# Page numbers of six quads kept, latents one group of four pages sooner, memory squares summed on VectorE, and a later scaling of key tiles

## The chip, the cores and the metric

The kernel runs on one core of a Trainium2 chip. The metric is device time in microseconds (us) of one run. The core has TensorE (PE; its weight loads are shown as PEld), VectorE (DVE), ScalarE (ACT), GpSimd (POOL), and SyncE (SP), which here issues the DMAs. Each engine takes its own instructions in order and waits on semaphores for the others.

## What is computed

One step of a hybrid decoder layer for two groups that share the weights: a prompt of 1024 tokens and 8 samples of 4 new tokens, each with 4096 past tokens in 32 pages of 128. The parts that matter here, cut:

```python
def mla_keys_values(ckv_n, kpe, pos, w_uk, w_uv, g_qk_k):
    k_nope = (ckv_n @ w_uk).reshape(*lead, MLA_HEADS, QK_NOPE)
    v = (ckv_n @ w_uv).reshape(*lead, MLA_HEADS, V_HEAD)
    k = qk_rope(rms_norm(jnp.concatenate([k_nope, k_pe], axis=-1), g_qk_k), pos)

def one(args):                      # a sample's attention over its pages
    c_all = jnp.concatenate([pool_ckv[pages].reshape(PAST_LEN, KV_LORA), c1], axis=0)
    pe_all = jnp.concatenate([pool_kpe[pages].reshape(PAST_LEN, QK_ROPE), pe1], axis=0)
    k, v = mla_keys_values(c_all, pe_all, k_pos, w_uk, w_uv, g_qk_k)
    return masked_attend(q1, k, v, q_pos, k_pos)

def mem_kv(mem, g_mem_in, w_mk, w_mv, g_mk):
    hm = rms_norm(mem, g_mem_in)    # 256 memory tokens of width 1024
    k = rms_norm((hm @ w_mk).reshape(n, m, MEM_HEADS, MEM_HEAD_DIM), g_mk)
    v = (hm @ w_mv).reshape(n, m, MEM_HEADS, MEM_HEAD_DIM)
```

Around these stand a spatial gating group beside the attention, one output projection, cross-attention into the memory and a gated feed-forward network with a short convolution.

## The kernel before

All products are float32, split into a high and a low part and done as three products (`mm3`, line 185; the casts are L200 on ACT and L201 on DVE, with a scale L204 and L207). In order of time: projections; attention of the prompt; attention of the samples over their pages; keys and values of the memory (`mem_kv`); output projection; cross-attention; feed-forward. In the two attention stages the order on PE, ACT, DVE and POOL is the order of the code (`manual_schedule`). On SP, and everywhere from `mem_kv` on, a scheduler sets it by its own simulation, so an edit can move instructions well away from it.

**Prompt attention.** Eight heads run in two halves of four. For each group of four token tiles (512 tokens) a list of steps, made by `proj_group` with `part` and the generator `norm` (L901 to L930), makes queries and keys: products, sums of squares, a reciprocal root (`rsqrt_steps`, L232 to L246 on DVE, L248 to L255 on POOL), the scale of the queries (L911), then that of the keys (L925 on DVE, L926 on POOL for the rope part). `head_prep` transposes four tiles of k, then of q, on PE (L949) and splits them into kTh, kTl, qTh, qTl. A unit of attention then computes scores s (L185), row maxima on DVE (L979, L983, L985), exponentials on ACT (L988), transposes of the weights pr on PE (L996), copies of them on ACT (L998), products with v (L1011). The lists `extra[t]` hang further work onto step t of the units: steps of `norm`, and sums of feed-forward weights (`weight_sums`, L831 to L843, on POOL, with DMAs on SP).

**Samples.** A step n covers two pages; a quad Q is four pages, so two steps. `quad_pages` reads a quad's four page numbers into registers of SP (TENSOR_LOAD and eight register operations); `quad_load` starts four DMAs of latents (cT, 3 buffers) and, apart from them, four of another layout of the same pages (ck, 15 buffers). POOL makes the rotated rope part krq from cT (`quad_rot`, L1347 to L1349), ACT and DVE or POOL make the high and low parts ch (L1358) and cl (L1362), PE multiplies krq (L1377) and computes scores. `quad_sums` squares the rope part of ck on ACT (L1370). `pages_ahead` starts the first quads during the prompt attention. `batch_softmax` runs in numbered parts r: L1423 scales the scores, L1426 and L1452 take the maximum, r = 9 is a PE transpose (L1455), r = 10 two DVE operations (L1458, L1460), r = 11 a PE product that spreads the maximum (L1463), an ACT copy bc (L1465) and DVE's subtraction (L1466), the last is the exponential (L1468). Products with the values follow in `quad_pv` (L1475, L1477).

**Memory.** `mem_kv` begins within the end of the last batch. It casts the memory (mh, ml), makes four heads of keys (L1545), sums of squares of the memory per token for its norm (L1558 on ACT and L1560 on POOL over 8 slices of 128x256, then one-column products, L1581), and values in four calls `values(k)`, k = 0, 2, 4, 6. `behind(a, b)` makes a stand after b in order without a wait.

**Feed-forward.** Products of quarters (`block`, tiles A, X, F, E in PSUM), with weights split by `weights` (L2090, L2091). The first block has within it the norm of the tokens: hr by a reciprocal root on DVE, transposed on PE (`half_row`, L2044), copied by ACT (L2047). The tile A has two buffers, which `half_row` and the copy a of A (L2146) share.

Of the kernel before, what the change touches and what calls it, by code (L numbers as in the profile page):

```python
# [154 lines left out]
class Net:  # L155
# [502 lines left out]
    def phase2a(self):  # L658
# [86 lines left out]
        sums = [(i, z) for i in (NK, NK + 1, *range(NK)) for z in range(2)]  # L745
        times = (1, 2, 3, 4, 5, 7, 8, 9, 11, 12, 14, 15, 16, 25, 26, 27, 29, 30, 36, 37, 39, 40, 41, 43, 44, 46)
        for t, x in zip(times, sums):
# [19 lines left out]
        with tc.manual_schedule(engines={E.PE, E.Activation, E.DVE, E.Pool}):  # L767
# [9 lines left out]
            for f in norm[:2]:  # L777
                f()
            extra[0][:0] = norm[2:]
            extra[1][:0] = v1[3:]  # L780
            steps, outs, pend, V = [], {}, [], []
# [85 lines left out]
    def proj_group(self, p, pp, hf, i0, i1, s, c, tt=("tp", 4)):  # L867
# [32 lines left out]
        def norm():  # L900
# [4 lines left out]
            nc.vector.tensor_tensor(rk, rk, c["kss"][:tn, i0:i1].unsqueeze(2).broadcast_to([tn, m, 4]), ALU.add)  # L905
            rf = r.rearrange("p m z h -> p (m z h)")
            yield from self.rsqrt_steps(p, rf, rf, 1.0 / 96)
            yield
# [25 lines left out]
        it = norm()  # L934
        return [alloc] + qk + [lambda: next(it, 0)] * 6, [lambda i=i: part(i, 2) for i in range(i0, i1) if i < 8]

# [184 lines left out]
    def pages_ahead(self):  # L1121
# [8 lines left out]
        yield  # L1130
        self.quads = {Q: self.quad_load(None, Q) for Q in range(3)}
        self.rvs = {Q: self.quad_pages(Q) for Q in (3, 4)}
        yield
# [5 lines left out]
    def phase2b(self):  # L1139
# [74 lines left out]
        def steps(n0, n1):  # L1214
            for n in range(n0, n1):
                Q, v = n // 2, n - 16 - LAG
                if n >= 10 and n % 2 == 0 and Q + AHEAD < NB * 8:
                    quads[Q + AHEAD] = self.quad_load(p, Q + AHEAD)
# [13 lines left out]
                if n % 2 and 0 <= Q + 2 < NB * 8:  # L1232
                    self.quad_rot(Q + 2, quads[Q + 2], cosT, sinT)
                if n in (-1, 1, 3, 5, 7):
                    k = Q + 4
                    rvs[k] = rvs.get(k) or self.quad_pages(k)
                    quads[k] = self.quad_load(None, k, None, rvs[k])
                for k in {1: (0,), 3: (5, 1), 4: (2,), 5: (3,), 6: (4,), 8: (6, 7)}.get(n, ()):
                    self.quad_load(p, k, quads[k], rvs.get(k))
# [279 lines left out]
    def mem_kv(self, raws, wk0):  # L1519
# [7 lines left out]
        mh, ml = (self.t(p, [P, 8, 256], FR, x) for x in ("mh", "ml"))  # L1527
        acc = self.t(p, [P, 256], F32, "acc")
        mr = [r.rearrange("p (k n) -> p k n", k=4) for r in raws[1:3]]
# [3 lines left out]
        for h in range(4):  # L1533
# [20 lines left out]
            yield  # L1554
        for k in range(8):
            x = mr[k // 4][:, k % 4]
            s2 = acc if k == 0 else self.t(p, [P, 256], F32, "msq", 2)
            nc.scalar.activation(s2, x, AF.Square)  # L1558
            if k:
                nc.gpsimd.tensor_tensor(acc, acc, s2, ALU.add)  # L1560
        yield
        av = [self.t(pp, [P, 512], F32, f"v{i}") for i in range(2)]

        def values(k):
            wh, wl = (x.rearrange("p k n -> p (k n)").rearrange("p (k n) -> p k n", k=2) for x in self.stream(I["w_mv"][k // 2], 8))
            for i in range(2):
                t = slice(i * P, i * P + P)
                x = self.mm3(av[i], [tuple(x[:, t] for x in xs[k + e]) for e in range(2)],
                             [(wh[:, e], wl[:, e]) for e in range(2)], first=k == 0, last=k == 6)
                if k == 6 and i == 0:  # L1570
                    self.behind(x, self.spread)
# [8 lines left out]
        for i in range(2):  # L1580
            nc.tensor.matmul(st[:, 8 + i : 9 + i], acc[:, i * P : i * P + P], self.ones[:, :1], start=True, stop=True)  # L1581
        rt = self.t(p, [P, 2], F32, "rt")
# [872 lines left out]
```

## Time and profile before

| | |
|---|---|
| median of three runs | 1844.83 us (1842.12 to 1846.34) |
| the profiled execution | 1843.82 us, span 1842.1 us |
| mean granted clock of PE in it | 0.994 |
| prompt attention, about | 196 to 403 us |
| samples, about | 403 to 861 us |
| memory keys and values, about | 861 to 905 us |
| start of the feed-forward network, about | 1165 us |

Times in the trace are us from the span's start. A row of the timeline has start, length, engine, line, operation, output<-input and, in brackets, how long the engine was idle before it and what ended that. Several equal neighbours are one row with their count; matmuls overlap, so their lengths add up to more than their time. PEclk is the granted clock of TensorE as a share of full speed.

### The profile page before, as it was taken

The numbers are of one execution on the slowest core, as the hardware profiler recorded it, in microseconds if no ns is written. First come the engines' busy times: TensorE is split into PE (matmuls) and PEld (weight loads), VectorE is DVE, ScalarE is ACT, GpSimd is POOL, SyncE is SP. The second block draws the span as 40 slices with busy tenths as digits, with TensorE's granted clock in tenths as the row PEclk, the third lists the DMA queues.
The fourth block names the chain that finished last, engine by engine and source line by source line (L and its number), as shares of the span: only waits on it lengthen the run. The fifth ranks groups of instructions, "written<-read, shape, count | busy, mean of one in ns | idle before, by whom it ended". The sixth has DMA issues, their size and how long they took to land.

```text
span 1842.1 us, 39314 instructions
## 1 busy us (share of the span) xinstructions
PE 1809.4 (98%) x14222; PEld 1706.1 (93%) x14222; DVE 1354.1 (74%) x2805; ACT 922.9 (50%) x1916; POOL 697.1 (38%) x852
## 2 busy tenths in 40 slices
PE   9999999999999999999999999999999999999999
PEld 8999777779999999998899979999999999999999
DVE  7855767757778776786645666898888888878664
ACT  7435667766555555555433556533333333444442
POOL 1021555634444444453123110277766777400000
PEclk9999999999999999999999999999999999999999
DMA  8101353557767666654555155222222222495242
GB/s 324 42 25 66 109 194 109 183 167 210 222 191 194 193 176 188 181 168 145 160 161 181 62 179 169 98 82 70 93 82 70 70 82 75 140 328 173 78 154 77
DMA packets 153187, 261.18 MB, mean 142 GB/s; under 512 B 20897, under 2 KB 97538, under 8 KB 152994
## 3 DMA queue, kind: packets, MB, share of 16 engines
q1 hardware_dynamic: 152130, 257.63, 44.8%
q8 instruction: 112, 1.84, 0.4%
q10 hardware_dynamic: 864, 1.05, 0.2%
q14 instruction: 81, 0.66, 0.1%
HBM read 212.79 MB, written 45.82 MB: 140 GB/s over the span
## 4 chain that ended last, share of the span: by engine, by line
PE 73%; DVE 5%; issue 4%; ACT 2%; POOL 2%; DMA 1%; SPq 1%; DVEq 0%; POOLq 0%; ACTq 0%
PE s L185 16%; PE d L185 12%; PE b L185 8%; PE F L185 7%; PE E L185 7%; PE X L185 7%; PE A L185 3%; PE y L185 2%; PE o L1011 2%; PE tp L996 1%; PE tp L185 1%; PE o L1477 1%; PE tp L949 1%; PE t L185 1%; ACT pr L988 1%
## 5 line engine op out<-in xcount | busy, mean ns | idle before, releaser
L185 PE MATMUL s<-w2h,ch 128*128 128x288 f32 (+1 forms) x1024 | 304.4, 297 | 0.5 <-ACT S L1380 0.5
L185 PE MATMUL s<-w2h,cl 128*128 128x288 f32 (+1 forms) x1024 | 296.5, 290 | 3.3 <-POOL cl L1362 2.3
L185 PE MATMUL s<-w2l,ch 128*128 128x288 f32 (+1 forms) x1024 | 295.3, 288 | 0.0
L185 PEld LDWEIGHTS s<-w2h,ch 128*128 128x128 f32 x1024 | 193.3, 189 | 9.0 <-issue 2.5
L185 PEld LDWEIGHTS s<-w2h,cl 128*128 128x128 f32 x1024 | 193.1, 189 | 5.2 <-POOL cl L1362 3.9
L185 PEld LDWEIGHTS s<-w2l,ch 128*128 128x128 f32 x1024 | 193.5, 189 | 0.0
L1405 DVE TENSOR_REDUCE ss<-sq 128x16 f32<-128x1024 f32 x128 | 155.3, 1214 | 33.4 <-ACT sq L1402 33.0
L1362 POOL TENSOR_TENSOR cl<-cT,ch 128x512 fp32r<-128x512 f32 x64 | 83.8, 1310 | 126.7 <-ACT ch L1358 118.0
L1402 ACT ACTIVATE sq<-s 128x512 f32<-128x512 f32 x128 | 76.5, 598 | 89.5 <-PE s L185 89.5
L1399 ACT ACTIVATE sq<-s 128x512 f32<-128x512 f32 x128 | 76.7, 599 | 75.3 <-PE s L185 74.7
L200 ACT CAST a<-brb 128x528 fp32r<-128x528 f32 x77 | 48.8, 634 | 109.1 <-PE d L185 102.8
L185 PE MATMUL d<-a,w 128*128 128x264 f32 x768 | 95.2, 284 | 0.0
L185 PEld LDWEIGHTS d<-a,w 128*128 128x128 f32 x768 | 94.3, 188 | 0.0
L201 DVE TENSOR_TENSOR a<-brb,a 128x528 fp32r<-128x528 f32 x77 | 54.3, 707 | 53.7 <-ACT a L200 53.7
L2091 POOL TENSOR_TENSOR lo<-s,hi 128x1024 fp32r<-128x1024 f32 x20 | 63.8, 3190 | 45.7 <-ACT hi L2090 45.7
L185 PE MATMUL mm<-whi,xh 128*128 128x256 f32 (+3 forms) x272 | 77.2, 285 | 0.0
L185 PE MATMUL mm<-wlo,xh 128*128 128x256 f32 (+3 forms) x272 | 76.9, 285 | 0.1
L185 PE MATMUL mm<-whi,xl 128*128 128x256 f32 (+3 forms) x272 | 76.8, 286 | 0.0
L2146 ACT COPY a<-A 128x264 f32<-128x264 f32 x43 | 16.1, 374 | 118.4 <-PE A L185 114.4
L1358 ACT CAST ch<-cT 128x512 fp32r<-128x512 f32 x128 | 73.4, 626 | 2.1 <-DMA cT<-cT 2.1
L2212 POOL TENSOR_TENSOR cv<-cv,row 128x1056 f32<-128x1056 f32 x22 | 64.9, 2952 | 19.0 <-ACT cv L2211 19.0
L185 PE MATMUL d<-a,hi 128*128 128x264 f32 x552 | 72.0, 284 | 0.0
(746 smaller groups left out, 6350.3 us busy)
## 6 DMA issues: line engine op xcount, KB each, us to landing
cT<-cT SPq DMA_DIRECT2D x256, 160.0 KB, 2.7
ck<-ck SPq DMA_DIRECT2D x256, 144.0 KB, 3.3
raw<-w_up SPq DMA_DIRECT2D x44, 512.0 KB, 3.5
wsumd<-wsum SPq DMA_DIRECT2D x26, 512.0 KB, 3.6
actd<-cv SPq DMA_DIRECT2D x44, 264.0 KB, 2.3
brb<-actd SPq DMA_DIRECT2D x44, 264.0 KB, 5.7
wsum<-w_down SPq DMA_DIRECT2D x22, 512.0 KB, 3.4
raw<-wsumd SPq DMA_DIRECT2D x20, 512.0 KB, 3.6
```

Of the source, the lines that this page charges most:

```text
L185: x = self.nc.tensor.matmul(out, l, r, start=first and i == 0, stop=last and i == len(seq) - 1)
L200: first = {"act": nc.scalar.copy, "pool": nc.gpsimd.tensor_copy, "dve": nc.vector.tensor_copy}[eng](hi, src)
L201: low = lambda: nc.vector.tensor_tensor(lo, src, hi, ALU.subtract)
L949: nc.tensor.transpose(tp[:, j * P : j * P + P], s[x, g * 4 + j][:, h % 4], self.ident)
L1011: nc.tensor.matmul(u["o"][g : g + 64, o : o + m * P], s["v"][:, j, h % 4], th[:, z * P : (z + m) * P], start=j == 0, stop=b == len(banks) - 1,
L1358: nc.scalar.copy(d["h"][:, k], src[k])
L1362: (nc.vector if k else nc.gpsimd).tensor_tensor(d["l"][:, k], src[k], d["h"][:, k], ALU.subtract)
L1399: nc.scalar.activation(sq[:, 0], ps[:, :, n0 : n0 + 256], AF.Square)
L1402: nc.scalar.activation(sq[:, 1], pt.rearrange("p (e d) -> p e d", e=2), AF.Square)
L1405: yield lambda: nc.vector.tensor_reduce(s["ss"][:, g0 : g0 + 2].rearrange("p e (z h) -> p z e h", z=2), sq.rearrange("p z e (h d) -> p z e ...
L2091: eng.tensor_tensor(lo, src, hi, ALU.subtract)
L2212: nc.gpsimd.tensor_tensor(cv, cv, row, ALU.mult)
```

## The change

Five edits:

1. The first five weight sums of the prompt attention are hung one step later.
2. `norm` has one step more, between the sums and the reciprocal root. Of the second group (tokens 512 to 1023 of the first half) three steps now go to `extra[0]`, and what is left, the scaling of the key tiles, to `extra[1]`.
3. `pages_ahead` reads the page numbers of quads 0 to 5, and they are kept. Before, it read those of 0 to 4, and those of 0, 1 and 2 were read again for their ck.
4. Latents of quads 8, 9 and 10 are entered at n = 9, 11 and 13, no longer at 10, 12 and 14, and the ck of quads 5 to 10 are spread over n = 7 to 14.
5. In `mem_kv` ACT squares the memory in place, 128x1024 at a time, and DVE sums four slices in one reduction each; the two sums are added in PSUM by two more one-column products. The values of k = 4, no longer of k = 6, stand behind the spread of the maximum.

```diff
-        times = (1, 2, 3, 4, 5, 7, 8, 9, 11, 12, 14, 15, 16, 25, ...
+        times = (2, 3, 4, 5, 6, 7, 8, 9, 11, 12, 14, 15, 16, 25, ...
...
-            extra[0][:0] = norm[2:]
-            extra[1][:0] = v1[3:]
+            extra[0][:0] = norm[2:5]
+            extra[1][:0] = norm[5:] + v1[3:]
...
+            yield
             yield from self.rsqrt_steps(p, rf, rf, 1.0 / 96)
...
-        return [alloc] + qk + [lambda: next(it, 0)] * 6, ...
+        return [alloc] + qk + [lambda: next(it, 0)] * 7, ...
...
-        self.quads = {Q: self.quad_load(None, Q) for Q in range(3)}
-        self.rvs = {Q: self.quad_pages(Q) for Q in (3, 4)}
+        self.rvs, self.quads = {}, {}
+        for Q in range(6):
+            self.rvs[Q] = self.quad_pages(Q)
+            if Q < 3:
+                self.quads[Q] = self.quad_load(None, Q, None, self.rvs[Q])
...
-                if n >= 10 and n % 2 == 0 and Q + AHEAD < NB * 8:
+                if n >= 16 and n % 2 == 0 and Q + AHEAD < NB * 8:
...
-                if n in (-1, 1, 3, 5, 7):
+                if n in (-1, 1, 3, 5, 7, 9, 11, 13):
...
-                for k in {1: (0,), 3: (5, 1), 4: (2,), 5: (3,), 6: (4,), 8: (6, 7)}.get(n, ()):
+                for k in {1: (0,), 3: (1,), 4: (2,), 5: (3,), 6: (4,), 7: (5,), 9: (6,), 11: (7,), 12: (8,), 13: (9,), 14: (10,)}.get(n, ()):
                     self.quad_load(p, k, quads[k], rvs.get(k))
...
-        acc = self.t(p, [P, 256], F32, "acc")
+        acc = [self.t(p, [P, 256], F32, f"acc{z}") for z in range(2)]
...
-        for k in range(8):
-            x = mr[k // 4][:, k % 4]
-            s2 = acc if k == 0 else self.t(p, [P, 256], F32, "msq", 2)
-            nc.scalar.activation(s2, x, AF.Square)
-            if k:
-                nc.gpsimd.tensor_tensor(acc, acc, s2, ALU.add)
+        for x, s2 in zip(mr, acc):
+            nc.scalar.activation(x, x, AF.Square)
+            nc.vector.tensor_reduce(s2, x.rearrange("p k n -> p n k"), AX.X, ALU.add)
...
-                if k == 6 and i == 0:
+                if k == 4 and i == 0:
                     self.behind(x, self.spread)
...
-            nc.tensor.matmul(st[:, 8 + i : 9 + i], acc[:, i * P : i * P + P], self.ones[:, :1], start=True, stop=True)
+            for z in range(2):
+                nc.tensor.matmul(st[:, 8 + i : 9 + i], acc[z][:, i * P : i * P + P], self.ones[:, :1], start=z == 0, stop=z == 1)
```

The order of the instructions at three places. Line numbers of the changed kernel are up to 4 higher than before. First DVE in the prompt attention, from the scale of the queries (L911) of the second group to the low parts of its transposes; k is the key tile, pr and nm the masked scores and their row maximum. Before:

```order
L911 TENSOR_TENSOR rq_2427<-hr_2593,sq_tok_69 128x4x4
L925 TENSOR_TENSOR k_2594<-k_2594,hr_2593 128x8x64 x2
L979 ISA pr_432_2873,nm_2874<-s_2875,cmask_2419 128x384
L979 ISA nm_2874 128x1
L985 TENSOR_SCALAR nm_2874<-nm_2874,rq_2427 128x1
L979 ISA pr_435_2881,nm_2882<-s_2883,cmask_2419 128x512
L979 ISA nm_2882 128x1
L985 TENSOR_SCALAR nm_2882<-nm_2882,rq_2427 128x1
L201 TENSOR_TENSOR kTl_2710<-tp_2918,kTh_2709 96x512
L207 SCALAR_TENSOR_TENSOR qTl_2925<-tp_2926,ggq_2422,qTh_2924 96x512
```

And now:

```order
L912 TENSOR_TENSOR rq_2427<-hr_2593,sq_tok_69 128x4x4
L980 ISA pr_432_2870,nm_2871<-s_2872,cmask_2419 128x384
L980 ISA nm_2871 128x1
L986 TENSOR_SCALAR nm_2871<-nm_2871,rq_2427 128x1
L980 ISA pr_435_2878,nm_2879<-s_2880,cmask_2419 128x512
L980 ISA nm_2879 128x1
L986 TENSOR_SCALAR nm_2879<-nm_2879,rq_2427 128x1
L926 TENSOR_TENSOR k_2594<-k_2594,hr_2593 128x8x64 x2
L201 TENSOR_TENSOR kTl_2710<-tp_2910,kTh_2709 96x512
L207 SCALAR_TENSOR_TENSOR qTl_2917<-tp_2918,ggq_2422,qTh_2916 96x512
```

The scaling of the key tiles has moved behind the two maxima. Next DVE in `mem_kv`; lo are low parts of weights, S the scores of the last batch, ss their factor, mx the maximum, dg and bc its spread. Before:

```order
L201 TENSOR_TENSOR lo_14646<-raw_14643,hi_14645 128x1024
L201 TENSOR_TENSOR lo_14745<-raw_14742,hi_14744 128x1024
L201 TENSOR_TENSOR lo_14763<-raw_14760,hi_14762 128x1024
L1423 TENSOR_TENSOR S_12857<-S_12857,ss_12858 128x256
L201 TENSOR_TENSOR lo_14827<-raw_14824,hi_14826 128x1024
L1426 TENSOR_REDUCE mx_14401<-S_12857 128x32
L1452 TENSOR_TENSOR mx_14401<-mx_14401 128x32
L201 TENSOR_TENSOR lo_14881<-raw_14878,hi_14880 128x1024
L1458 TENSOR_REDUCE mm_14565<-m_14563 32x1
L201 TENSOR_TENSOR lo_14921<-raw_14918,hi_14920 128x1024
L1460 TENSOR_SCALAR dg_14567<-ident_60,mm_14565 32x32
```

And now:

```order
L201 TENSOR_TENSOR lo_14536<-raw_14533,hi_14535 128x1024
L1561 TENSOR_REDUCE acc_2105_14385<-ck_14160 128x256
L1561 TENSOR_REDUCE acc_2106_14386<-ck_14250 128x256
L201 TENSOR_TENSOR lo_14617<-raw_14614,hi_14616 128x1024
L1427 TENSOR_TENSOR S_12746<-S_12746,ss_12747 128x256
L201 TENSOR_TENSOR lo_14635<-raw_14632,hi_14634 128x1024
L1430 TENSOR_REDUCE mx_14290<-S_12746 128x32
L1456 TENSOR_TENSOR mx_14290<-mx_14290 128x32
L201 TENSOR_TENSOR lo_14701<-raw_14698,hi_14700 128x1024
L1462 TENSOR_REDUCE mm_14455<-m_14453 32x1
L1464 TENSOR_SCALAR dg_14457<-ident_60,mm_14455 32x32
```

The two reductions stand ahead of a weight cast; the low part of the next weight now comes after L1423 (L1427 there), and the subtraction (L1470 there) no longer follows the root of the memory's norm. Last PE in the same stage, where m<-ident,mx is the transpose of the maximum and m<-dg,ones its spread; v are the memory's values. Before, the end of `values(2)` and what follows it (the spread stands 17 rows further on, between the products of `values(6)`):

```order
L185 MATMUL v_2143_14741<-lo_14763,mh_14494 128x512
L185 MATMUL v_2143_14741<-hi_14762,ml_14495 128x512
L1579 MATMUL st_14493<-ones_61,sq_14606 128x1 x2
L1579 MATMUL st_14493<-ones_61,sq_14641 128x1 x2
L1579 MATMUL st_14493<-ones_61,sq_14676 128x1
L1455 MATMUL m_14563<-ident_60,mx_14401 32x128
L1579 MATMUL st_14493<-ones_61,sq_14676 128x1
L1581 MATMUL st_14493<-ones_61,acc_14496 128x1 x2
L185 MATMUL v_2142_14740<-hi_14826,mh_14494 128x512
```

And now, the transpose between the products of `values(0)`:

```order
L185 MATMUL v_2137_14613<-lo_14617,mh_14383 128x512
L185 MATMUL v_2137_14613<-hi_14616,ml_14384 128x512
L185 MATMUL v_2137_14613<-hi_14616,mh_14383 128x512
L1459 MATMUL m_14453<-ident_60,mx_14290 32x128
L185 MATMUL v_2137_14613<-lo_14617,mh_14383 128x512
L185 MATMUL v_2137_14613<-hi_14616,ml_14384 128x512
```

and, behind the twelve products of `values(2)`, the spread between the sums:

```order
L1580 MATMUL st_14382<-ones_61,sq_14496 128x1 x2
L1580 MATMUL st_14382<-ones_61,sq_14531 128x1 x2
L1467 MATMUL m_14459<-dg_14457,ones_61 128x32
L1580 MATMUL st_14382<-ones_61,sq_14566 128x1 x2
L1583 MATMUL st_14382<-ones_61,acc_2105_14385 128x1
L1583 MATMUL st_14382<-ones_61,acc_2106_14386 128x1
```

Both have moved ahead, the transpose by fourteen products of the values and the spread by eighteen. On SP the loads of cT for quads 6 to 10 now stand ahead of some loads of ck that they followed, with four readings of page numbers fewer among them, and at the start of the feed-forward network the scheduler puts the first transposes of hr (L2044) 35 products further back.

More of the change, by code (lines that the diff above doesn't have):

```diff
@@ L745, in phase2a @@
         sums = [(i, z) for i in (NK, NK + 1, *range(NK)) for z in range(2)]
-        times = (1, 2, 3, 4, 5, 7, 8, 9, 11, 12, 14, 15, 16, 25, 26, 27, 29, 30, 36, 37, 39, 40, 41, 43, 44, 46)
+        times = (2, 3, 4, 5, 6, 7, 8, 9, 11, 12, 14, 15, 16, 25, 26, 27, 29, 30, 36, 37, 39, 40, 41, 43, 44, 46)
         for t, x in zip(times, sums):
@@ L934, in proj_group @@
         it = norm()
-        return [alloc] + qk + [lambda: next(it, 0)] * 6, [lambda i=i: part(i, 2) for i in range(i0, i1) if i < 8]
+        return [alloc] + qk + [lambda: next(it, 0)] * 7, [lambda i=i: part(i, 2) for i in range(i0, i1) if i < 8]
     def head_prep(self, p, pp, h, s, c):
```

## The prediction

> **What bounds the kernel now.** I read the page first.
>
> ```profile
> span 1842.1 us, 39314 instructions
> PE 1809.4 (98%) x14222; PEld 1706.1 (93%) x14222; DVE 1354.1 (74%) x2805; ACT 922.9 (50%) x1916; POOL 697.1 (38%) x852
> ```
>
> TensorE (PE) is busy for 1809.4 of 1842.1 us, and the change takes no product away. It can only win what PE waits, and what PE loses when its clock is lowered. So the waits of PE come next (engine, line, what it waited for, total, times, longest); these four lie where the change works.
>
> ```profile
> PE o L1475 <- ACT S L1468: 2.3, 1, 2.3
> PE s L1377 <- POOL krq L1349: 2.3, 2, 1.8
> PE A L2044 <- DVE hr L246: 1.8, 1, 1.8
> PE m L1455 <- DVE mx L1452: 0.8, 1, 0.8
> ```
>
> No wait is longer than 2.3 us. Then I cut the trace into stretches around the waits, for the clock that was granted (columns: stretch, length, busy time and count of PE, PEld, DVE, ACT, POOL, then PEclk, DMA share, GB/s).
>
> ```profile
> 211.00:215.00 4.00, 1.93 (x10) 1.00 (x9) 2.15 (x5) 3.23 (x7) 3.69 (x6) 1.00 0.38 131
> 215.00:222.00 7.00, 7.00 (x26) 5.42 (x25) 4.22 (x15) 0.03 (x1) 1.11 (x2) 0.51 0.54 170
> 256.00:259.40 3.40, 2.32 (x18) 2.06 (x17) 1.64 (x7) 2.60 (x7) 2.92 (x4) 1.00 0.46 147
> 454.00:457.40 3.40, 1.61 (x14) 1.37 (x13) 2.96 (x7) 2.32 (x5) 2.40 (x4) 0.99 0.56 153
> 457.40:460.80 3.40, 3.40 (x17) 3.40 (x16) 3.40 (x4) 0.60 (x1) 3.32 (x5) 0.50 0.88 251
> 876.40:881.40 5.00, 5.00 (x23) 4.05 (x22) 0.46 (x3) 3.26 (x6) 4.35 (x9) 1.00 0.35 105
> 880.60:884.00 3.40, 2.58 (x21) 2.35 (x20) 3.01 (x5) 1.71 (x2) 0.32 (x2) 1.00 0.22 34
> 884.00:887.40 3.40, 3.40 (x11) 2.72 (x11) 3.12 (x13) 0.00 (x0) 0.00 (x0) 0.50 0.70 235
> 890.90:894.30 3.40, 1.17 (x6) 0.59 (x4) 3.06 (x14) 1.75 (x2) 0.00 (x0) 0.99 0.57 183
> 894.30:897.70 3.40, 3.32 (x32) 3.08 (x36) 0.79 (x4) 2.39 (x6) 0.00 (x0) 0.50 0.23 87
> 1173.60:1179.60 6.00, 6.00 (x51) 6.00 (x51) 3.10 (x3) 3.97 (x7) 0.88 (x2) 1.00 0.02 4
> ```
>
> Behind a 3.4 us stretch with 1.8 us or more of PE idle stands one at half clock: behind 457.4 and 894.3 for 3.4 us, behind 215.0 for 7 us. At 256.0 to 259.4 PE was idle 1.08 us and the clock stayed. At 880.6 to 884.0 0.82 us were idle, and half clock followed; there the trace has many one-column products, which may count little. At half clock half of the work is lost: 1.7 us behind each short one, 3.4 us behind 215.0. So a removed wait is worth itself, and 1.7 us more where it causes a dip.
>
> The Trainium skill ("TensorE: Matmul & The Clock Gate", the section on why this matters for kernels) sets the bar higher: avoid idle gaps over about 3 us, since one idle window halves the clock. The rows differ: dips here stand behind 0.8 to 2.3 us. By that rule only the idle time would be won, which is the first rival below.
>
> **The change, part by part.** Each sum is made against the profiled execution, 1843.82 us; that is 1.0 under the shown median of 1844.83.
>
> *Key tiles of the second token group (L925).* Moved behind the two row maxima of 384 and 512 columns (L979).
>
> ```profile
> 207.58 2.69 DVE L925 TENSOR_TENSOR k<-k,hr 128x512 f32<-128x512 f32 x2
> 210.01 0.73 PE L949 MATMUL tp<-ident,k 128*96 128x128 f32 x4
> 211.63 0.21 DVE L985 TENSOR_SCALAR nm<-nm,rq 128x1 f32<-128x1 f32 x1
> 213.16 0.68 ACT L204 ACTIVATE qTh<-tp,ggq 96x512 fp32r<-96x512 f32 x1
> 213.89 0.41 PE L185 MATMUL s<-kTh,qTh 96*128 96x320 f32 x1 [0.73 <-ACT qTh L204]
> ```
>
> The two maxima, which now stand between the end of L925 at 210.27 and the end of L985 at 211.84, come 2.7 us sooner, so the exponentials (L988) behind them and the waits of L996 for these fall. But the transposes of k (L949) read what L925 writes. It now ends the 1.6 us of the maxima later, at 211.9, and PE, in order, waits at L949 in place of L996. The last k transpose is then out at about 212.3, q's at 212.9, the two ACT casts end at 213.55: the scores start 0.3 us sooner than 213.89. L925 ran beside POOL work and may be shorter: 0.5. I take +0.4. The idle time is spread over 210.1 to 213.6, on both sides of the window edge at 211.6 (3.4 before 215.0), so the dip behind 215.0 may go (3.4 more) or stay; I leave it in the sum and give it to the range. Bounds: -0.5 to +3.9.
>
> The later groups have one more step each, so that three small DVE operations (L903 to L905, 0.6 us the first and an estimated 1.2 the three) come ahead of maxima that PE waits for, at two places.
>
> ```profile
> 292.67 0.60 DVE L903 TENSOR_TENSOR hr<-hr,sq_tok 128x16 f32<-128x16 f32 x1
> ```
>
> PE has slack of a few tenths there: -0.3, bounds -1.5 and 0. The five weight sums that are entered one step later keep their place on POOL and SP: 0.
>
> *Pages kept, latents sooner.*
>
> ```profile
> 415.35 0.59 SPq L1221 DMA_DIRECT2D ck<-b  x1
> 417.65 1.91 SPq L1330 DMA_DIRECT2D cT<-cT  x4
> 419.75 2.72 SPq L1334 DMA_DIRECT2D ck<-ck  x4
> 443.37 0.50 ACT L1370 ACTIVATE ksq<-ck 128x128 f32<-128x128 f32 x2
> 448.43 1.93 SPq L1330 DMA_DIRECT2D cT<-cT  x4
> 454.93 0.61 POOL L1347 TENSOR_TENSOR krq<-cT,cosT 128x128 f32<-128x128 f32 x1 [5.84 <-DMA cT<-cT]
> ```
>
> SP is one queue. A load of four pages takes 2.1 us of it (417.65 to 419.75), a reading of page numbers the 1.7 us from 415.94 to 417.65. Ahead of the latents (cT) of quad 8, issued at 448.43, four re-readings go (quads 0, 1, 2 and 5: 6.8 us), and the key load (ck) of quad 5 and one or two others move behind: some 8 to 12 us sooner, less where a buffer isn't free yet. POOL waited 5.84 us for quad 8's latents and PE 1.79 of them; both krq waits (2.3) go, and the dip behind 457.4 (1.7). Sum 4.0; I take 3.9, bounds 1.5 (an SP stall eats half) to 4.0. What is late next: ck of quad 5, read by L1370 at 443.37. It was issued at 419.75; now it goes behind quad 7's latents, an estimated 433 to 435, and lands near 438. ACT has 5 us in hand.
>
> *Memory squares.* Seven POOL additions, eight ACT squares go; two ACT squares of 128x1024 in place and two DVE reductions come.
>
> ```profile
> L1560 POOL TENSOR_TENSOR acc<-acc,msq x7: 727/734/741, 871.6 to 879.9; 128x256 f32<-128x256 f32 x7
> 599.62 1.22 DVE L1405 TENSOR_REDUCE ss<-sq 128x16 f32<-128x1024 f32 x1 [0.23 <-ACT sq L1402]
> 599.67 0.46 POOL L1348 TENSOR_TENSOR krq<-cT,sinT 128x128 f32<-128x128 f32 x1
> 867.78 1.39 POOL L249 TENSOR_TENSOR rqa<-rqa,rqx 128x64 f32<-128x64 f32 x1
> 880.95 0.43 DVE L1423 TENSOR_TENSOR S<-S,ss 128x256 f32<-128x256 f32 x1 [4.54 <-POOL ss L255]
> 883.10 0.19 DVE L1452 TENSOR_TENSOR mx<-mx 128x32 f32<-128x32 f32 x1
> 890.06 0.40 PE L1463 MATMUL m<-dg,ones 32*128 32x32 f32 x2
> 893.24 1.08 ACT L1468 ACTIVATE S<-S 128x1056 f32<-128x1056 f32 x1 [0.45 <-DVE rqh L245]
> 894.38 0.64 PE L1475 MATMUL o<-cn,S 128*32 128x257 f32 x1 [2.31 <-ACT S L1468]
> ```
>
> The additions stand between the small steps of POOL's reciprocal root; 7 x 0.73 = 5.1 us sooner its result reaches L1423: 875.8 instead of 880.95. A POOL step of 128x64 took 1.39 beside a DVE subtraction (the casts' low parts, L201), one of twice the size 0.46 within a DVE reduction; so the new reductions should not slow the chain. They are unpriced: the nearest row is 1.21 to 1.22 for 128x1024, strided an estimated double; at 2.4 each they still end by 875, ahead of the cast that values(0) needs. From L1423 to the maximum are 2.3 us: it is there at 878.1, and PE comes to the moved L1455 at 878.2 (8 products of 0.22 behind 876.4). The 0.82 us and the dip behind 884.0 go. PE then reaches the spread (L1463) at 882.2, ahead of the 24 last products (24 x 0.23 = 5.6 us) and 0.8 of small ones. From the spread to the exponential's start were 3.2 us (890.06 to 893.24); so much again and 1.08 make 886.5, and PE needs it at 888.6. So 2.31 us go, and the dip behind 894.3: 0.8 + 2.3 + 2 x 1.7 = 6.5, less 0.2 for two more one-column products: 6.3. Bounds: 1 (L1455 waits 2 us and dips) to 6.5.
>
> *Start of the gated network.* Its order shifts too: the first transposes of hr go behind 35 products more, 0.12 us each (51 in 6.0 us), 4.2 us; hr comes about 1 us later. The 1.84 us wait goes.
>
> ```profile
> 1171.90 1.48 PE L2044 MATMUL A<-ident,hr 128*128 128x128 f32 x10 [1.84 <-DVE hr L246]
> 1177.90 1.05 ACT L2090 CAST hi<-s 128x1024 fp32r<-128x1024 f32 x1 [0.33 <-PE A L185]
> ```
>
> But a copy of A (L2146), whose buffer the second transposes need, now stands on ACT behind a cast that waits for A's own products: an estimated 0.7 us of new wait. +1.1, bounds -2 and +1.8.
>
> Sum: 0.4 - 0.3 + 3.9 + 6.3 + 1.1 = 11.4; 1843.8 - 11.4 = **1832.4 us**.
>
> **Rivals.** (1) *Idle goes, dips stay*: the four dips return in other windows, since the steps left between small products may suffice. Against it: 256.0 to 259.4 kept its clock with 1.08 us idle. Then 0.1 + 2.3 + 2.9 + 1.1 = 6.4: 1837.4. By the rule of the Trainium skill named above (same page, same section) it is this one. (2) *The memory chain is late*: strided reductions hold DVE or POOL; PE waits at L1455 for 2 us and dips; the end gains 1 in place of 6.3: 1837.7. (3) *Slower*: ck of quads 5 to 10, now issued 4 to 8 steps nearer to their use, land late. L1370 then holds ACT's queue, the latents' casts behind it (L1358) and so the scores. It decides at 5 us of lateness for quad 5 against my estimate; with 2 us lost on each of six quads and a dip each, 6 x 3.7 = 22.2 against 7.5 of other gains: 1858.5. (4) *It doesn't do it*: latents wait for free buffers, and dips elsewhere pay back the rest: 1842 to 1845.
>
> **How the numbers follow.** Forecast 0.62, (1) 0.13, (2) 0.12, (4) 0.08, (3) 0.05. The low end has the 215.0 dip gone (1829.0), bounds of 1 us and 1.5 of scatter as in the runs shown: 1826.5. The high end takes (1) and (2) with the lower bounds of the first and last part (3 us): 1841. Over 0.2% (3.7 us, what a measurement of this kernel can tell from no change) faster: forecast, (1) and (2) less a little, 0.85; within 0.09; slower 0.06.
>
> **What would show it.** Right: no wait at L1377 and L1475, none or under 0.5 at L1455, full clock after 457, 884 and 894; PE idle near 20 us; a new wait of PE at L949 near 210 to 212. Wrong: POOL still waits over 4 us for cT between 436 and 455, L1370 ends ACT idle time, half clock stays at 884 or 894, or PE waits over 2 us at the second hr transposes.

## The result, and the profile after

| | before | after |
|---|---|---|
| median, measured together | 1845.59 us (1842.12 to 1846.75, 4 runs) | 1832.46 us (1831.72 to 1835.1, 4 runs) |
| ratio, 95% interval | | 0.9937 [0.9921, 0.9954] |
| profiled execution: time, span | 1843.82, 1842.1 us | 1835.1, 1833.4 us |
| its PE idle (span less busy) | 32.7 us | 27.4 us |
| its time at half clock, tail left out | 20.4 us | 13.6 us |

Faster by 0.6%; the forecast was 1832.4. A dip, below, is a stretch in which PE's granted clock is half. The profiled execution of after is the slowest of the four. For that pair of profiles the account closes: 5.3 us less idle, and 6.8 us less at half clock, of which half is lost (3.4), make the 8.7 us between the spans. The head of the page:

```profile
span 1833.4 us, 39288 instructions
PE 1806.0 (99%) x14226; PEld 1702.6 (93%) x14226; DVE 1352.0 (74%) x2807; ACT 921.9 (50%) x1910; POOL 695.7 (38%) x845
```

PE's waits in after, as in the prediction's second fence (total, times, longest):

```profile
PE s L185 <- DVE pr L984: 4.0, 6, 1.4
PE s L185 <- POOL cl L1366: 3.4, 8, 1.1
PE tp L950 <- DVE k L926: 1.5, 2, 0.8
PE st L343 <- DMA xr<-xT: 0.7, 1, 0.7
```

The four waits that the change was aimed at (L1475, L1377, L2044 and L1455 of before) are gone. New are 1.5 us at the transposes of k, as announced, up to 1.1 us in one wait for the latents' low parts cl, and 0.7 at the start, where nothing was changed.

The clock, in windows of after as in the prediction's third fence:

```profile
210.70:214.10 3.40, 1.94 (x14) 1.24 (x12) 2.23 (x6) 2.24 (x7) 3.17 (x4) 1.00 0.02 5
214.10:217.50 3.40, 2.62 (x12) 1.78 (x12) 2.71 (x8) 0.90 (x2) 3.01 (x5) 1.00 0.45 154
217.50:224.30 6.80, 6.80 (x25) 5.15 (x24) 3.80 (x14) 1.90 (x4) 1.02 (x2) 0.50 0.53 168
454.40:457.80 3.40, 2.30 (x19) 2.06 (x17) 3.40 (x5) 1.20 (x2) 3.36 (x3) 1.00 1.06 315
457.80:461.20 3.40, 3.39 (x27) 3.39 (x28) 3.33 (x6) 2.15 (x5) 3.02 (x6) 1.00 1.00 249
876.30:879.70 3.40, 3.40 (x25) 3.07 (x24) 1.62 (x2) 1.13 (x2) 0.00 (x0) 0.99 0.84 253
879.70:886.50 6.80, 6.80 (x19) 5.54 (x20) 4.55 (x19) 1.51 (x2) 0.00 (x0) 0.50 0.30 93
```

The dips behind 235, 457 and 894 are gone. The first of these stands in no row of the prediction; here it is in before:

```profile
235.40:238.80 3.40, 3.40 (x13) 1.60 (x11) 2.56 (x11) 0.00 (x0) 2.20 (x3) 0.51 0.53 185
```

The one at 215 is there still, 7 us long. Near 880 stands a dip of 6.8 us behind a window in which PE was never idle: that was in no part of the prediction.

The timeline of after at the key transposes:

```profile
210.90 0.21 DVE L986 TENSOR_SCALAR nm<-nm,rq 128x1 f32<-128x1 f32 x1
211.03 1.82 DVE L926 TENSOR_TENSOR k<-k,hr 128x512 f32<-128x512 f32 x2
211.85 0.40 PE L950 MATMUL tp<-ident,k 128*96 128x128 f32 x2 [0.81 <-DVE k L926]
212.90 0.42 PE L950 MATMUL tp<-ident,k 128*96 128x128 f32 x2 [0.65 <-DVE k L926]
214.58 0.42 PE L185 MATMUL s<-kTh,qTh 96*128 96x320 f32 x1 [0.38 <-ACT qTh L204]
```

The scaling now comes behind the maxima, and takes 1.82 us for the two in place of 2.69. The transposes wait for it, and the scores start at 214.58. This execution was about 1 us behind that of before by then (0.7 of it the wait at the start), so they start some 0.3 us sooner.

The latents, on SP's queue, POOL and PE (L1366 is L1362 of before, L1351 is L1347):

```profile
437.77 1.94 SPq L1334 DMA_DIRECT2D cT<-cT  x4
445.89 0.58 POOL L1351 TENSOR_TENSOR krq<-cT,cosT 128x128 f32<-128x128 f32 x1
454.44 2.08 POOL L1427 TENSOR_TENSOR S<-S,ss 128x768 f32<-128x768 f32 x1 [7.00 <-DVE ss L246]
457.81 0.40 PE L185 MATMUL s<-w2h,cl 128*128 128x288 f32 x1 [1.11 <-POOL cl L1366]
```

Quad 8's latents are issued at 437.77, 10.7 us sooner than 448.43, and POOL takes them at 445.89 with no wait, where it stood idle for 5.84 us. What is late next isn't ck of quad 5 but POOL itself: L1427 waits for DVE's factor ss, takes 2.08 us, and the low parts cl queue behind it.

The memory in after:

```profile
866.31 3.93 DVE L1561 TENSOR_REDUCE acc<-ck 128x256 f32<-128x1024 f32 x2
867.58 0.32 POOL L255 TENSOR_TENSOR rqy<-rqh,rqy 128x64 f32<-128x64 f32 x1
871.62 0.43 DVE L1427 TENSOR_TENSOR S<-S,ss 128x256 f32<-128x256 f32 x1 [0.22 <-POOL ss L255]
873.80 0.19 DVE L1456 TENSOR_TENSOR mx<-mx 128x32 f32<-128x32 f32 x1
874.14 0.27 PE L1459 MATMUL m<-ident,mx 128*32 128x128 f32 x1
877.54 0.95 PE L1580 MATMUL st<-ones,sq 128*128 128x1 f32 x8
881.64 1.08 ACT L1472 ACTIVATE S<-S 128x1056 f32<-128x1056 f32 x1 [2.43 <-DVE rqx L232]
889.01 0.40 PE L1479 MATMUL o<-cn,S 128*32 128x257 f32 x1
```

The chain runs as the prediction had it: the maximum ends at 873.99 and its transpose takes no wait at 874.14; the exponential ends at 882.7 and the last products, at 889.01, take none. And the start of the gated network:

```profile
1174.56 0.39 PE L2046 MATMUL A<-ident,hr 16*128 16x16 f32 x2 [0.40 <-ACT a L2148]
```

The wait of 1.84 us has become one of 0.40, for the copy of A.

### The profile page after: what moved, and what is told of

It is laid out like the page before. It is cut to its first block, busy times and chain, and to the rows that moved or that the text cites. A ratio compares the mean times of both kernels' runs of the same rounds, so it can differ in the third digit from the quotient of the medians.

```text
span 1833.4 us, 39288 instructions
## 1 busy us (share of the span) xinstructions
PE 1806.0 (99%) x14226; PEld 1702.6 (93%) x14226; DVE 1352.0 (74%) x2807; ACT 921.9 (50%) x1910; POOL 695.7 (38%) x845
## 3 DMA queue, kind: packets, MB, share of 16 engines
q8 instruction: 112, 1.84, 0.4%
## 4 chain that ended last, share of the span: by engine, by line
PE 73%; issue 4%; DVE 4%; DMA 2%; SPq 2%; ACT 2%; POOL 1%; DVEq 0%; POOLq 0%; ACTq 0%
PE s L185 15%; PE d L185 12%; PE b L185 8%; PE F L185 7%; PE X L185 7%; PE E L185 7%; PE A L185 3%; PE y L185 3%; PE o L1012 2%; PE tp L997 1%; DMA ck<-ck 1%; PE o L1481 1%; DMA cT<-cT 1%; SPq L1334 1%; PE tp L185 1%
## 5 line engine op out<-in xcount | busy, mean ns | idle before, releaser
L1366 POOL TENSOR_TENSOR cl<-cT,ch 128x512 fp32r<-128x512 f32 x64 | 83.3, 1302 | 134.8 <-ACT ch L1362 110.0
L1362 ACT CAST ch<-cT 128x512 fp32r<-128x512 f32 x128 | 73.4, 626 | 0.2 <-issue 0.2
```

Of the source, the lines that this page charges most:

```text
L1362: nc.scalar.copy(d["h"][:, k], src[k])
L1366: (nc.vector if k else nc.gpsimd).tensor_tensor(d["l"][:, k], src[k], d["h"][:, k], ALU.subtract)
```

## The experiments

The theory: the gain is idle time of PE that goes (memory, latents, gated network) and half clock that goes with it. The rivals: one part carries it all, or the idle time only moves and the rest is chance of the clock. Two figures serve throughout. One is the length of a stage in the profiled execution, between landmarks on PE: *samples* from the first page scores to the memory's first keys product, *memory* from there to the first cross-attention product with diag (L1600 of before), *end* from the start of the gated network to the last instruction. The other is the clock's share: (1 - mean clock) times the time of each run, averaged. It counts half of all half-clock time as lost, which is not always so (see The clock). The clock has three places (1.8 us), so only means of many runs carry it. Line numbers differ by up to 4 between the kernels.

| kernel | runs | median us | ratio to before, 95% | mean clock | samples | memory | end |
|---|---|---|---|---|---|---|---|
| before | 48 | 1843.2 | 1 | 0.9948 | 458.2 | 38.2 | 675.8 |
| only_mem | 6 | 1837.2 | 0.9971 [0.9959, 0.9983] | 0.9960 | 455.4 | 33.5 | 674.0 |
| only_loads | 11 | 1840.65 | 0.9984 [0.9975, 0.9993] | 0.9949 | 455.1 | 38.2 | 674.0 |
| only_prompt | 11 | 1842.19 | 0.9996 [0.9987, 1.0005] | 0.9964 | 455.9 | 38.1 | 675.8 |
| wide_sums | 5 | 1834.8 | 0.9955 [0.9942, 0.9969] | 0.9986 | 455.1 | 32.0 | 677.1 |
| spread_k6 | 5 | 1833.69 | 0.9943 [0.993, 0.9956] | 0.9982 | 454.8 | 33.4 | 674.0 |
| mixed_wide | 5 | 1831.03 | 0.9934 [0.9921, 0.9947] | 0.9994 | 454.8 | 32.0 | 674.0 |
| before_pages | 12 | 1844.6 | 1.0012 [1.0002, 1.0021] | 0.9942 | 459.8 | 36.7 | 674.0 |
| after_pages | 6 | 1832.3 | 0.9945 [0.9932, 0.9959] | 0.9985 | 454.8 | 31.9 | 674.0 |
| after_again | 5 | 1832.45 | 0.994 [0.9926, 0.9953] | 0.9986 | 455.1 | 31.9 | 674.1 |
| scale_split | 5 | 1832.77 | 0.994 [0.9927, 0.9954] | 0.9990 | 454.8 | 31.9 | 674.0 |
| mixed_again | 5 | 1830.78 | 0.9936 [0.9922, 0.9949] | 0.9990 | 454.8 | 32.0 | 674.0 |
| pages_wide | 5 | 1832.05 | 0.9939 [0.9925, 0.9952] | 0.9988 | 455.1 | 32.0 | 674.5 |

(The stages of before are those of the profile shown in the prediction; after's own are 455.1, 35.0 and 674.0.)

### One part at a time, on the kernel before

**only_mem**: the memory edits alone (the fifth edit of the change).

```diff
+        for x, s2 in zip(mr, acc):
+            nc.scalar.activation(x, x, AF.Square)
+            nc.vector.tensor_reduce(s2, x.rearrange("p k n -> p n k"), AX.X, ALU.add)
...
-                if k == 6 and i == 0:
+                if k == 4 and i == 0:
```

> Only the memory part (squares in place, DVE reductions, values of k = 4 behind the spread) on the kernel before. My account: PE's waits at the maximum's transpose (0.82 us) and at the last products (2.31) go, and with the scheduler's new order at the start of the feed-forward network the 1.84 there falls to about 0.4, so PE idle falls from 28.8 to about 24.3 us; the half clock behind 894 goes with its wait. 4.6 us by idle time alone, up to 8 with two dips: 1837.5 to 1841. Rival (dips come back elsewhere): 4.6 and no more, about 1841. Rival (the reductions delay the maximum): a wait over 1 us at the transpose of the maximum and under 3 us of gain.

The largest part: 5.8 us by the means (1842.92, that of the runs of before beside it, to 1837.11), just under the 1837.5 to 1841 that was expected. The waits for the maximum and for the exponential are gone, and the transposes of hr go late in this kernel too, as expected; the end is 1.8 us shorter. One thing was not foreseen: its samples stage is 2.8 us shorter than in the profile of before, with the old loads.

**only_loads**: the pages kept, latents sooner, ck spread (edits 3 and 4).

```diff
+        for Q in range(6):
+            self.rvs[Q] = self.quad_pages(Q)
...
-                if n in (-1, 1, 3, 5, 7):
+                if n in (-1, 1, 3, 5, 7, 9, 11, 13):
```

> Only the kept page numbers and the latents one group sooner, on the kernel before. My account: both krq waits (0.46 and 1.79 us) go, a wait of about 1.1 for cl near 457 takes the place of one, and the half clock behind 457 goes: 1.4 us of idle time and 1.7 of clock, 3.1 in all, about 1842. Rival (key loads now late): ACT idle before ksq and PE idle over 3 us between 440 and 460, slower than before. Rival (idle only): about 1843.5.

2.8 us by the means, of which the end's 1.8 is again the late place of hr, which was not expected here. The krq waits and the dip behind 457 are gone, but of the 3.1 us that they were to give only about 1.0 is left, and no clock was won: 0.9949 against 0.9950 in the runs of before beside it.

**only_prompt**: weight sums one step later, the extra step, the later scaling (edits 1 and 2).

```diff
-            extra[0][:0] = norm[2:]
-            extra[1][:0] = v1[3:]
+            extra[0][:0] = norm[2:5]
+            extra[1][:0] = norm[5:] + v1[3:]
```

> Only the later key scaling, the extra step and the five shifted weight sums, on the kernel before. My account: PE waits at the key transposes (about 0.8 and 0.65 us) in place of the exponentials; the scores start 0.3 us sooner; the wait near 234 falls from 1.8 to 0.4 us and one near 290 grows from 0.15 to 1.3. Idle in all the same within 0.5 us: 1844 to 1846, or 1.7 less where the half clock behind 235 goes. Rival (this part carries the gain): over 4 us faster.

No change of the time that can be measured (0.5 us by the means, interval -0.7 to 1.7), though the mean clock is 0.9964 against 0.9950 in the runs of before beside it. The waits at the key transposes came as expected, and a new one for the queries' low parts:

```profile
242.89 0.33 PE L185 MATMUL s<-kTh,qTl 96*128 96x128 f32 x1 [1.40 <-DVE qTl L207]
```

The hr transposes stay early, and their 1.8 us wait stays. In this kernel, too, there are no krq waits. POOL took quad 8's latents at 452.82 in only_mem, at 451.17 in only_prompt, and at 454.93 in the profile of before; the issue on SP's queue was at 447.75, 445.87 and 448.43. Rows of only_mem and only_prompt:

```profile
452.82 0.57 POOL L1347 TENSOR_TENSOR krq<-cT,cosT 128x128 f32<-128x128 f32 x1 [4.76 <-DMA cT<-cT]
451.17 0.47 POOL L1348 TENSOR_TENSOR krq<-cT,cosT 128x128 f32<-128x128 f32 x1 [5.39 <-DMA cT<-cT]
```

From the issue to POOL's start went 6.5 us in before, 5.1 in only_mem and 5.3 in only_prompt. In these two POOL finished krq at 454.35 and 452.81, and PE took it at 454.50 and 452.86. So with the old loads the latents land just when PE needs them: by 1.4 us or less the wait comes or doesn't. The 2.3 us of krq waits, and the dip, from which the prediction took its price, are those of one execution.

The three means add up to 9.1 us under before, with the end's 1.8 in two of them, so 7.3; the whole change gives 9.8 (spread_k6) to 11.2 (after_again) against the runs of before beside it. The other 2.5 to 4 us are in no part alone. Each mean is uncertain by 0.3 to 0.7 us (one standard error), and the three parts share their runs of before, so that the sum is uncertain by nearly 3 us: that the parts help each other is not shown, and the runs don't assign the rest.

### Are the latents early enough, or were they late by accident?

**before_pages** and **after_pages**: the same four unused readings of page numbers on SP, in the kernel before and in the changed one.

```diff
+                if n in (6, 8):
+                    self.quad_pages(n)
+                    self.quad_pages(n)
```

> The kernel before with four more readings of page numbers on SP (1.7 us each), two ahead of quad 7's latents and two ahead of quad 8's; nothing uses them. If late latents are what the loads part cures, krq waits of PE grow to 3 to 7 us near 445 to 460 with half clock behind: the stretch from the first page scores to the memory (455.4 to 458.2 us in the runs so far) takes 460 to 466. Rival (the latents have slack, and the wait was one run's accident): it stays at 455 to 458. The scheduler also puts the first hr transposes late here, worth 1.8 us.

> The same four readings added to the changed kernel. My account: its latents land 8 us or more sooner, so they take the 7 us with little or no wait, at most 2 us in the same stretch: 455 to 457, in all 1830 to 1836. Rival (the gain was the fewer readings on SP, not the earlier place): the same loss as in the kernel before, 5 us or more.

PE in before_pages, then PE in after_pages at the same place:

```profile
458.60 0.80 PE L1380 MATMUL s<-bd,krq 128*128 128x128 f32 x2 [3.83 <-POOL krq L1352]
```

```profile
455.62 0.40 PE L185 MATMUL s<-w2h,cl 128*128 128x288 f32 x1 [1.07 <-POOL cl L1369]
```

In the kernel before, quad 8's issue falls from 448.43 to 451.96, PE waits 3.83 us with half clock behind it, and the samples take 459.8 us, a hair under the 460 that was expected. The median rises by 1.4 us although the hr transposes are late and give 1.8. In the changed kernel the same readings cost nothing: 454.8 us, the wait for cl as without them, 1832.3 us. So the loads part is real. It takes the latents from the edge to 5.6 us of slack in after (POOL ends krq at 447.44, PE takes it at 453.01); in after_pages 3.3 us of it are left (447.56 and 450.85), though POOL waits 2.36 us for the latents there. What that is worth depends on where the execution stood: 3.1 us against the profile of before, 0.3 to 0.8 against the stages of only_mem and only_prompt.

### Which part of the memory edit?

**spread_k6**: the changed kernel with the values of k = 6 behind the spread, as before.

```diff
-                if k == 4 and i == 0:
+                if k == 6 and i == 0:
```

> The changed kernel without one edit: the values of k = 6, as before, stand behind the spread. The scheduler gives the same order of instructions on every engine as for the changed kernel, so both accounts say that this edit is worth nothing: 1830 to 1835, clock loss about 4 us as in the changed kernel's runs. If the edit mattered at all, a wait of over 1 us at the last products would show.

The order of instructions is the same and so is the time: that edit is worth nothing, and this kernel and after_again are ten more runs of the changed kernel. What moves the spread forward is that the maximum is ready sooner.

### The clock

**wide_sums**: the twelve products that sum the squares, and write one column each, write 128 equal ones.

```diff
-                nc.tensor.matmul(st[:, 2 * h + i : 2 * h + i + 1], sq[h][:, i * P : i * P + P], self.ones[:, :1], ...
+                nc.tensor.matmul(st[:, 2 * h + i : 2 * h + i + P], sq[h][:, i * P : i * P + P], self.ones[:, :P], ...
```

> The changed kernel with the twelve one-column sums of squares in the memory part made 128 columns wide: each writes 127 columns more, which the next ones overwrite and nothing reads; the same number of products. The scheduler then puts the first hr transposes of the feed-forward network back where they were before, which may bring back up to 1.4 us of wait there. If products of one column count little for the clock: no half clock behind 877 to 880, and the mean granted clock is over the changed kernel's by 0.001 to 0.002, so the time stays at 1831 to 1833 in spite of the wait. If the half clock there comes by chance or from idle time: it stays, and the time rises by about 1.4 us to 1834.

The memory stage takes 32.0 us and no dip stands in it, as the first account said. But the mean clock is 0.9986 against 0.9984 of the changed kernel's ten runs, not 0.001 to 0.002 over it, and the median doesn't fall, since in this kernel the scheduler puts the hr transposes early again: a wait of 1.8 us and a dip behind it, 3.1 us in the end stage (677.1). So the width had to be tried with hr late, in **pages_wide** (after_pages with the same widths). It was run beside **after_again**, the changed kernel as it is.

> The changed kernel with the four unused readings of after_pages, which cost nothing there, and the one-column sums 128 columns wide; the scheduler leaves the first hr transposes late here. My account (one-column products can lower the clock): memory stage 32 to 32.5 us, clock loss 1 to 2 us less than the changed kernel's mean, 0.4 us of wider products: 0 to 1.5 us under the changed kernel. Rival (the width is of no matter): 0.4 us over it.

> The changed kernel as it is, beside the three others of this call. 1830 to 1835, clock loss 3 to 4 us; half clock in the memory stage (1.7 to 3.4 us lost there) in some executions and not in others, as in the runs so far.

pages_wide is 0.2 us under after_again by the means, with an interval from 1.5 under to 1.1 over: neither account falls. The clock loss of after_again, 2.6 us, is under the 3 to 4 expected. What the traces show of the memory stage, windows of only_mem, of spread_k6 and of wide_sums:

```profile
879.70:883.10 3.40, 3.40 (x24) 3.12 (x24) 2.32 (x3) 1.13 (x2) 0.00 (x0) 1.00 0.64 197
883.10:886.50 3.40, 3.40 (x10) 2.61 (x9) 2.81 (x19) 1.48 (x2) 0.00 (x0) 0.50 0.40 114
```

```profile
878.60:882.00 3.40, 3.40 (x27) 3.19 (x26) 0.49 (x1) 0.99 (x2) 0.00 (x0) 1.00 0.81 261
882.00:885.40 3.40, 3.40 (x10) 2.64 (x9) 3.14 (x8) 0.96 (x3) 0.00 (x0) 0.50 0.26 57
```

```profile
877.90:881.30 3.40, 3.40 (x24) 3.01 (x23) 2.74 (x5) 1.06 (x3) 0.00 (x0) 1.00 0.65 169
881.30:884.70 3.40, 3.40 (x17) 2.71 (x16) 2.11 (x11) 2.14 (x3) 0.00 (x0) 1.00 0.29 104
```

In only_mem and spread_k6, as in after, half clock follows a window in which PE was busy throughout, but with the one-column products. Among kernels with the new memory edits and one-column products the dip is in the profiles of after, only_mem and spread_k6, and not in those of after_pages, after_again and scale_split; with wide ones it is in none of four. That points to the narrow products without proving it: three of six against none of four.

**mixed_wide** and **mixed_again** (the same kernel twice): wide sums, half of the second group's key scaling on POOL, and the extra step only in groups of the first half of the heads. **scale_split** has the last two without the wide sums.

```diff
-            for a, eng in ((slice(0, m // 2), nc.vector), (slice(m // 2, m), nc.gpsimd if hf else nc.vector)):
+            for a, eng in ((slice(0, m // 2), nc.vector), (slice(m // 2, m), nc.gpsimd if hf or i0 == 4 else nc.vector)):
...
-            yield
+            if not hf:
+                yield
```

> The changed kernel, and three more edits: the second half of the second group's key scaling on POOL, the extra step only in the groups of the first half of the heads, and the one-column sums 128 columns wide. The late place of the first hr transposes stays here. My account: the second wait at the key transposes (0.65 us) goes, the wait near 290 falls from 1.3 to about 0.2, no half clock near 880; against that about 0.4 us of wider products: 2 to 5 us under the changed kernel, 1827 to 1830, memory stage near 32 us. Rival (POOL and DVE get in each other's way at the key scaling): the wait at the key transposes stays at 1.4 us or more, and only the 3 us of the clock are won.

> The same kernel as mixed_wide, now beside the changed kernel: 1 to 4 us under it. If the difference to the changed kernel was only one between calls, it is within 0.5 us here.

> The changed kernel, with two edits of the key scaling alone: the second half of the second group's on POOL, and the extra step only in the groups of the first half of the heads. The one-column sums stay. My account (what was won over the changed kernel is the wait of 0.65 us at the key transposes, and less half clock near 215): 0.5 to 2 us under the changed kernel. Rival (all was won by the wider sums): the same as the changed kernel within 0.5 us.

The key transposes of mixed_wide, and the POOL half of the scaling:

```profile
212.09 0.61 PE L951 MATMUL tp<-ident,k 128*96 128x128 f32 x4 [1.17 <-DVE k L927]
```

```profile
209.35 1.04 POOL L927 TENSOR_TENSOR k<-k,hr 128x512 f32<-128x512 f32 x1 [10.40 <-DVE hr L246]
```

The second wait at the transposes is gone, but the first grows from 0.81 to 1.17, so 0.3 us are won there, and the wait near 290 falls to 0.9, not to 0.2. PE's waits as a whole hardly fall. Over all its runs this kernel is 1.7 us under the changed one (mean 1831.18 of ten against 1832.84 of ten, interval 0.4 to 2.9); by themselves the five runs beside after_again give 1.0, the least that was expected, with an interval that holds 0. Its medians are the lowest here, 12 us under before. scale_split is 0.4 us under after_again, a little less than expected, with an interval of over 1 us to both sides: whether its edits or the wider sums bring the 1.7 isn't settled.

Three profiled executions have a granted clock of 1.000: those of mixed_wide, after_pages and scale_split. All three show the same row:

```profile
core 0: 1828.2 us, clock 1.000
```

Three kernels that differ at the key scaling, in the sums and on SP have one span when no dip falls. It is not a floor: one run of scale_split spanned 1827.7 us. Nor do spans differ by half of the dips' length. The profile of mixed_again has a dip of 6.8 us and spans only 0.6 us more than that of mixed_wide, the same kernel, 1828.8 us. Its dip, and a wait of mixed_wide that it hasn't:

```profile
216.60:223.40 6.80, 6.80 (x25) 5.18 (x25) 3.92 (x13) 1.74 (x3) 1.29 (x2) 0.50 0.59 193
```

```profile
243.43 0.33 PE L185 MATMUL s<-kTh,qTl 96*128 96x128 f32 x1 [1.07 <-DVE qTl L207]
```

From the first scores near 214 to those near 288 mixed_wide takes 73.9 us and mixed_again 74.6; after_pages, without the dip, 73.4, and pages_wide, with it, 75.4. So this dip costs 0.7 to 2.0 us and not the 3.4 that the prediction put on it: with the dip PE waits less behind it. In the memory stage, where next to no waits are left, the dips cost about half of their length: 1.5 us (only_mem, spread_k6) and 3.1 us (after) over the 31.9 of after_again. Where dips fall is not fixed by the order of instructions. Windows of after_again, and one of after_pages:

```profile
254.60:258.00 3.40, 1.95 (x13) 1.50 (x11) 2.48 (x7) 2.23 (x6) 2.43 (x4) 1.00 0.52 170
258.00:261.40 3.40, 3.40 (x14) 2.02 (x13) 1.60 (x8) 0.00 (x0) 1.36 (x3) 0.50 0.90 302
```

```profile
255.00:258.40 3.40, 1.95 (x11) 1.27 (x12) 3.07 (x10) 1.29 (x4) 2.25 (x4) 1.00 0.53 184
```

The same 1.45 us of PE idle, in the same order: in after_again half clock follows it (and none stands near 215), in after_pages there is none at all, in after it stands at 217.5 and not at 258, in spread_k6 at 291.5. That would fit a window whose edges fall elsewhere in each execution, which either gathers the short waits or splits them. The edges can't be seen where no dip marks them, so this is argued and not shown.

## Why the prediction was right, step by step

**The total** (1832.4 against 1832.46) is closer than its terms. Set the 48 runs of before (mean 1843.1, clock 0.9948: 9.6 us lost to the clock) against the ten of spread_k6 and after_again (1832.8, 0.9984: 2.9 us). Of 10.3 us, 6.7 are clock and 3.6 the rest. The prediction had 6.3 of idle time and 5.1 of clock. Its idle terms were too large and its clock term too small; that they met within 0.1 us is luck. The 6.7 count half of all half-clock time as lost and are an upper estimate, since the dip behind 215 costs less than that.

**Key tiles, +0.4 and -0.3.** Right at the place: scores 0.3 us sooner, the two scalings shorter. The dip behind 215 was rightly kept out of the sum: it stayed in this profile and is missing in others. The 3.4 us put on it in the bounds were too much (0.7 to 2.0). Not seen: the wait near 234 fell from 1.82 to 0.41, that near 290 grew from 0.15 to 1.32 (inside its bound of -1.5), and near 243 one of up to 1.6 comes and goes. Alone the part gives 0.5 us, within the uncertainty.

**Pages and latents, +3.9.** The mechanism was right and the size off. The 2.3 us of waits and the 1.7 of their dip were real in the profile of before; the new wait for cl (1.1) takes some back, and the stage is 3.1 us shorter. But they were priced from one execution that happened to be late. The step that failed is "both krq waits (2.3) go, and the dip behind 457.4": other executions with the old loads hadn't them, and there the part is worth 0.3 to 0.8. The estimates for ck of quad 5 (issued at 433 to 435 and in time for L1370; it was issued at 433.13, and L1374 read it at 442.41 without a wait) and for the lead of quad 8 (8 to 12 us; 10.7) held, so rival (3) had no ground.

**Memory, +6.3.** Right in its idle part: 3.28 us of PE idle in that stage of before, 0.13 in after, against 0.8 + 2.3. The reductions took 1.97 us each against 2.4, and POOL's steps beside them 0.32 to 0.38, so they didn't slow the chain. The maximum came 0.15 us ahead of PE; the prediction had 0.1. The two dips went only in part: the one behind the exponential's wait is gone in every profile with this edit, the one near 884 comes back in half of those with one-column sums. The stage gained 3.1 us in after's profile, 4.7 in only_mem's and spread_k6's, 6.2 in those of after_pages and after_again. The prediction had noted that the window before 884 had many one-column products "which may count little" and then put the dip down to the 0.82 us wait; that was the mistake of this term, since with the wait gone the dip still comes in three profiles of six.

**Gated network, +1.1.** 1.8 us: the wait fell to 0.40, not 0.7, and the end stage from 675.8 to between 674.0 and 674.5 in every kernel with hr late. This gain comes from the scheduler's order, which flips with unrelated edits: with only_mem, only_loads and even four unused readings, not with only_prompt or wide_sums.

**The marks it set.** No wait at L1377 and L1475, none at L1455, full clock after 457 and 894, a new wait at L949: as it said. Wrong: half clock stood near 884, and PE idle "near 20 us" was too low (27.4 by span less busy time, 5.3 under before where 6.3 were summed). Rival (1), idle goes and dips stay, was the nearest one for the profiled execution (1835.1); for the mean it falls, since 10.3 us were won where it has 6.4, and the mean clock rose from 0.9948 to 0.9984. The Trainium skill's bar of about 3 us for an idle gap ("TensorE: Matmul & The Clock Gate", the section on why this matters for kernels) would have kept the clock out of it; no wait of PE here reached 3 us in any kernel but before_pages, and the dips came and went with shorter ones.

## What to carry to other kernels

A wait in one profile is one draw: before pricing its removal, see whether the same instruction waits in another execution, or put a small delay ahead of it and look whether it answers at once (here nearly 7 us of idle readings cost the old order about 3 us and the new one nothing). Look for half clock in the mean clock of many runs, not in the dips of one trace, and read what a dip costs from the length of its stage with it and without it: here one of 6.8 us cost 3.1 us where PE had next to no waits, and 0.7 to 2.0 where it had some. And where a scheduler decides the order, read the whole order for each variant: two unrelated experiments here won or lost 1.8 us at the far end of the kernel.

## What was not expected of the hardware

- Half clock came behind 3.4 us in which PE was never idle, when one-column products stood in them (876.3 to 879.7 in after, and the like in only_mem and spread_k6): in three profiles of six, and in none of four with the same products 128 columns wide, which is too few to prove it. It cost 1.5 or 3.1 us.
- The width itself cost little: the memory stage without a dip took 32.0 us in wide_sums and 31.9 in after_again, and the sums of squares took 0.280 us each 128 columns wide in wide_sums (2.5 us for 16), against 0.235 one column wide in after (2.1 for 16).
- A strided DVE reduction of 128x1024 to 128x256 took 1.97 us, against 1.22 for the contiguous one of an input of the same size (128x1024 to 128x16), and POOL's steps of 128x64 took 0.32 to 0.38 us beside it, where beside a DVE subtraction such a step took 1.39.
- One order of instructions gave spans of 1828.2 to 1833.4 us (after, spread_k6, after_again, and after_pages with its free readings): most of it by dips, but 1.3 us between after_pages and spread_k6 by the wait for qTl near 243 (0.22 and 1.56 us).
